# Softmax reciprocals of a chunked-attention block: transposed as 128x8 inside the probabilities' PSUM tile and spread over partitions by transfers on ScalarE's queue

## The chip, the core and the metric

The kernel runs on one core of one Trainium2 chip. The metric is the time of one execution in microseconds (us), measured on the device. TensorE (PE) multiplies and transposes into PSUM, VectorE (DVE) and ScalarE (ACT) work on PSUM and SBUF, GpSimd (POOL) works on SBUF, and SyncE (SP) issues almost all DMA transfers. In the program before the change ScalarE issues none.

## The reference

One layer: a shared input projection feeds a state-space mixer (SSM) and a chunked attention of 8 heads of 64; their outputs are normalised, projected and added, and a SwiGLU feed-forward layer follows. The part that matters here:

```python
scores = einsum(q, k) / sqrt(64) + bias          # each frame sees its 64-frame chunk and the 8 before
probs  = softmax(scores, axis=-1)
out    = einsum(probs, v)
```

The kernel leaves the probabilities unnormalised: it multiplies the exponentials with v and scales the product by one over the row sums afterwards.

## The kernel before, in words

The sequence of 2048 frames is cut into four blocks (`sb`) of 512. The eight heads are taken in four pairs (`pr`) of two (`hh`), and each head of a block in four query groups (`qp`) of 128 frames. That makes 128 steps, `steps[s] = (sb, pr, hh, qp)`. A pair ends with the step whose `(hh, qp)` is `(1, 3)`; this text calls that step b, and the place a boundary. There are 16 boundaries, named (block, pair) below.

In step s the loop at L1071 records, mostly in the order "sptf" (L1056/L1081):

- `scores` of step s (L937): the score matmuls into the PSUM tile `sc` (one buffer), the bias and row minimum on VectorE (L963, tile `mn`), and the exponential on ScalarE (L966), which also leaves the row sums in `sums` (tile `sm`).
- `pv_head` (L985), one step after the last transposes of a head: up to 16 matmuls of the transposed probabilities with v into a `pj` bank; ScalarE copies one half out (`yt`, L1006) and VectorE adds the other half into `ya` (L1007).
- `transp` of step s-2 (L970): up to five 128x128 transposes of the exponentials into the PSUM tile `pt`, of which there is one buffer; ScalarE rounds it out as `pth` (L982), and VectorE writes the remainder `ptl` (L983). The next step's transposes overwrite `pt`, so they wait for `ptl`.
- the background units ("f"): projections for q, k and v of the next block, the SSM and weight preparation, in small pieces between the steps. They keep PE busy. A planner spreads them over the steps by windows of steps.

PE's instructions stay in the order in which they are recorded. For the other engines a scheduler orders instructions when it builds the program; on the chip each engine then runs its list strictly in that order, and an instruction that waits holds up all that stand behind it.

At a boundary, before the change: at step b+3 `pv_head` takes the reciprocals of the 128x8 row sums (L993) and ScalarE writes them out 64 times each, as the 128x512 tile `rb` (L995). At step b+4 `pv_scale` (L1009) transposes `rb` by four 128x128 transposes into a `pj` bank (L1015), so that each reciprocal stands at its query's column on all 64 partitions of its head; VectorE multiplies `ya` by that bank (L1016), and SP stores `ya` to DRAM (L1017). On PE these four transposes stand directly ahead of the `pt` transposes of step b+4, which belong to probabilities of step b+2.

Transfers that SP and ScalarE issue share eight completion semaphores in rotation (DMAHW0 to DMAHW7 in the rows below). A transfer waits until the one before it on its semaphore has landed, whichever queue issued that.

Of the kernel before, what the change touches and what calls it, by code (L numbers as in the profile page):

```python
# [12 lines left out]
AF = mybir.ActivationFunctionType  # L13
# [91 lines left out]
def f32(ap):  # L105
    return ap.bitcast(F32)
# [629 lines left out]
def att_phase(k, ident, S, aw, x0, roots):  # L736

    tc, nc, io, pfs = k.tc, k.nc, k.io, k.pfs
    with ExitStack() as cx:
# [197 lines left out]
        def scores(st):  # L937
            sb, pr, hh, qp = st
            h = 2 * pr + hh
            if qp == 0:  # L940
                hd = st_head[sb, h] = Head()
                hd.nb = nbs.pop(h) if nbs else load_nb(h)
                hd.s = {}
                hd.p = None
            hd = st_head[sb, h]
            if qp == 1 and (sb, h) < (NSB - 1, H - 1):
                nbs[(h + 1) % H] = load_nb((h + 1) % H)
            q2h, q2l, k2 = qk[sb, pr][hh]
# [12 lines left out]
            if (hh, qp) == (0, 0):
                sums[sb, pr] = k.t(aa, "sm", [P, 2, 4], bufs=3)
            ins = nc.vector.tensor_tensor_reduce(  # L963
                s[:, :nk].rearrange("p (a b) -> p a b", a=nch), ps[:, :nch, :half],
                hd.nb[:, nk - 1 :: -1].rearrange("p (a b) -> p a b", a=nch), 1.0, 3e38, ALU.add, ALU.min, mn[:])
            nc.scalar.activation(s[:, :nk], s[:, :nk], AF.Exp, bias=mn[:], scale=-1.0, accum_out=sums[sb, pr][:, hh, qp : qp + 1])  # L966
            k.least = ins.ins
            hd.s[qp] = s, k0

        def transp(st):  # L970
            sb, pr, hh, qp = st
            hd = st_head[sb, 2 * pr + hh]
            if qp == 0:
                hd.p = k.t(aa, "pth", [P, 5, 4, P], F32R), k.t(aa, "ptl", [P, 5, 4, P], F32R)
            pth, ptl = hd.p
            s, k0 = hd.s.pop(qp)
            pt = k.t(psum, "pt", [P, 5, P], bufs=1)
            for kb in range(k0, qp + 5):
                k.ta.transpose(pt[:, kb % 5, :], s[:, (kb - k0) * P : (kb - k0 + 1) * P], ident[:])
            runs = [(0, 5)] if sb else ([(4, 5)] if qp == 0 else [(4, 5), (0, qp)])  # L980
            for a, b in runs:
                k.high = nc.scalar.copy(pth[:, a:b, qp, :], pt[:, a:b, :]).ins  # L982
                k.low = nc.vector.tensor_tensor(ptl[:, a:b, qp, :], pt[:, a:b, :], f32(pth[:, a:b, qp, :]), op=ALU.subtract).ins  # L983

        def pv_head(st):  # L985
            sb, pr, hh, _ = st
            h = 2 * pr + hh
            pth, ptl = st_head[sb, h].p
            if hh == 0:
                yas[sb, pr] = k.t(aa, "ya", [P, SB])  # L990
            if hh == 1:
                rs = k.t(aa, "rs", [P, 2, 4], bufs=2)
                nc.vector.reciprocal(rs[:], sums[sb, pr][:])  # L993
                rb = rbs[sb, pr] = k.t(aa, "rb", [P, 4, 2, HD])
                nc.scalar.copy(rb[:], rs[:].rearrange("p h i -> p i h").unsqueeze(3).to_broadcast([P, 4, 2, HD]))  # L995
            ya = yas[sb, pr]
            yp = k.t(psum, "pj", [P, 512], bufs=2)
            kbs = [4] + [kb for kb in (range(5, 8) if sb == 0 else (0, 1, 2, 3, 5, 6, 7))]
            for n, kb in enumerate(kbs):
                a, b = max(0, kb - 4), min(3, kb) + 1  # L1000
                vt = vts[4 * (sb - 1) + kb, h // 4][:, h % 4, :]
                for m, px in ((0, pth), (1, ptl)):
                    k.ta.matmul(yp[:, a * P : b * P], vt, px[:, kb % 5, a:b, :].rearrange("p a b -> p (a b)"),
                                     start=n == 0 and m == 0, stop=n == len(kbs) - 1 and m == 1)
            yt = k.t(aa, "yt", [P, SB])
            nc.scalar.copy(yt[:64], yp[64:128, :])  # L1006
            nc.vector.tensor_tensor(ya[hh * 64 : hh * 64 + 64, :], yp[0:64, :], yt[:64], op=ALU.add)  # L1007

        def pv_scale(st):  # L1009

            sb, pr, _, _ = st
            ya, rb = yas[sb, pr], rbs.pop((sb, pr))
            pb = k.t(psum, "pj", [P, 512], bufs=2)
            for i in range(4):
                k.ta.transpose(pb[:, i * P : (i + 1) * P], rb[:, i].rearrange("p h d -> p (h d)"), ident[:])  # L1015
            nc.vector.tensor_tensor(ya[:], ya[:], pb[:], op=ALU.mult)  # L1016
# [54 lines left out]
        for s in range(N + LAG + 2):  # L1071
# [9 lines left out]
            for o in TURNED.get(s % 32, ORDER) if s < N - 32 else ORDER:  # L1081
# [7 lines left out]
                        nc.gpsimd.tensor_copy(k.ys[GELU.index(s)].rearrange("p (c j) -> p c j", j=L), y[:, :, :64].rearrange("p j c -> p c j"))  # L1089
                elif o == "p" and LAG + 1 <= s < N + LAG + 1 and steps[s - LAG - 1][3] == 3:  # L1090
                    pv_head(steps[s - LAG - 1])
                elif o == "p" and s >= LAG + 2 and steps[s - LAG - 2][2:] == (1, 3):
                    pv_scale(steps[s - LAG - 2])
                elif o == "f":
                    for u in units[: None if s < GSTART else -1]:
                        u.advance(s)
# [853 lines left out]
def block_kernel(tc, io, phases="pusamf"):  # L1950
# [3 lines left out]
    with ExitStack() as cx:  # L1954
# [4 lines left out]
        def pp():  # L1959
# [1 line left out]

        S = {
            "u": k.t(dram, "u", [L, DS, NSB, NC // NSB]), "y": k.t(dram, "y", [L, DS, NC]),
            "ya": k.t(dram, "ya_s", [NSB, DS, SB]), "x1": k.t(dram, "x1", [D, SEQ]),
            "k": k.t(dram, "ks", [2, H, P, SB]), "nb": k.t(dram, "nbs", [H, 768]),
            "bst": k.t(dram, "bsts", [4, P, 8 * P]), "v": k.t(dram, "vs", [NPR, 2, 2, NS, 9 * CH]),
            "hc": k.t(dram, "hc", [2, 7, P, 4, 512]), "h": k.t(dram, "hs", [4, P, HALF]), "ws": k.t(dram, "wss", [12, P, 2, 1024]),
# [90 lines left out]
```

## Time and profile before

| | |
|---|---|
| median of 3 runs | 2187.09 us (2184.46 to 2187.53) |
| the profiled execution's own time | 2187.64 us |
| its span, first to last instruction | 2185.5 us |
| granted TensorE clock | 0.997 |
| attention steps | about 126 to 685 us of the span |

The profile is of one execution. Its span leaves 2.1 us of its own time outside. A row of a timeline gives the start in us from the span's start, the duration in us, engine, line, operation, output tile and input tiles, and the count; a bracket at the end gives idle time of that engine just before it and what ended that. A row of waits gives total, times and longest, in us. A row of a tile gives minimum, median and maximum duration in ns. Rows "SPq" are transfers on SP's queue; "to landing" is the time from a transfer's issue until all its data has arrived.

### The profile page before, as it was taken

Reading aid. Unit: us, or ns where it says so; the run is one execution under the profiler, and the core shown is the slowest. Engines: PE = TensorE matmul, PEld = TensorE weight load, DVE = VectorE, ACT = ScalarE, POOL = GpSimd, SP = SyncE. Lnnn points to the kernel's source line nnn. Section 1 sums busy time; section 2 is a strip of 40 time slices with the busy share of each in tenths; the row PEclk is TensorE's granted clock in tenths of the full one; section 3 lists DMA queues with packets and bytes.
Section 4 is the critical chain, followed back from the end, with each engine's and each line's share of the span. In section 5 each row is a group of like instructions: output and inputs, shape, how many; then the busy total and the mean of one; then the engine's idle time right before and its main releaser. Section 6 shows DMA issues by size and latency. Waiting matters only on the chain.

```text
span 2185.5 us, 30150 instructions
## 1 busy us (share of the span) xinstructions
PE 2144.4 (98%) x10606; PEld 1810.5 (83%) x10606; DVE 1535.0 (70%) x2680; ACT 1008.2 (46%) x1697; POOL 378.7 (17%) x849
## 2 busy tenths in 40 slices
PE   8998999999998999999999999999999999999998
PEld 7787898898887888888888888888888888888887
DVE  8767566666567667766776769766665587688785
ACT  7356466555586621533333345333333443353322
POOL 3367777676310000000000000000000100000000
PEclk9999999999999999999999999999999999999999
DMA  9788877965745346834554757555433476575552
GB/s 337 229 285 266 295 231 247 306 218 167 211 145 178 111 144 206 286 108 148 173 184 139 246 197 278 189 174 193 158 124 98 153 291 221 192 252 182 202 212 78
DMA packets 197592, 440.12 MB, mean 201 GB/s; under 512 B 20225, under 2 KB 37681, under 8 KB 190337
## 3 DMA queue, kind: packets, MB, share of 16 engines
q1 hardware_dynamic: 188816, 410.34, 56.1%
q0 software_dynamic: 8624, 27.86, 4.1%
q8 instruction: 83, 1.36, 0.3%
q14 instruction: 69, 0.56, 0.1%
HBM read 294.72 MB, written 135.29 MB: 197 GB/s over the span
## 4 chain that ended last, share of the span: by engine, by line
PE 89%; DVE 5%; DMA 2%; ACT 2%; issue 2%; SPq 0%; POOL 0%; DVEq 0%; ACTq 0%
PE X L83 22%; PE ps L83 22%; PE Y L83 11%; PE pf L83 10%; PE big L83 9%; PE W L83 5%; PE pj L83 4%; PE pt L86 2%; PE sc L83 2%; DVE ptl L983 1%; DVE w L182 1%; DVE lo L815 0%; DMA w<-wss 0%; DMA xt<-in_xp 0%; PE pp L83 0%
## 5 line engine op out<-in xcount | busy, mean ns | idle before, releaser
L83 PE MATMUL X<-hi,c 128*128 128x512 f32 x1408 | 448.9, 389 | 0.0
L83 PE MATMUL ps<-hd,hd 128*128 128x512 f32 (+1 forms) x1920 | 428.0, 384 | 0.0
L83 PEld LDWEIGHTS ps<-hd,hd 128*128 128x128 f32 x1920 | 353.4, 188 | 70.9 <-DVE hd L182 0.3
L83 PEld LDWEIGHTS X<-hi,c 128*128 128x128 f32 x1408 | 264.3, 188 | 55.2 <-DVE c L182 0.4
L83 PE MATMUL X<-lo,c 128*128 128x512 f32 x704 | 273.9, 389 | 0.0
L182 ACT CAST hd<-hd 128x1536 fp32r<-128x1536 f32 (+2 forms) x114 | 148.0, 1309 | 226.3 <-DMA hd<-hq 165.1
L83 PE MATMUL Y<-hi,c 128*128 128x512 f32 x696 | 222.2, 389 | 0.0
L182 DVE TENSOR_TENSOR hd<-hd 128x1536 fp32r<-128x1536 f32 (+2 forms) x114 | 174.8, 1539 | 32.3 <-ACT hd L182 31.9
L182 DVE TENSOR_TENSOR c<-S,c 128x512 fp32r<-128x512 f32 x175 | 120.2, 687 | 98.7 <-ACT c L182 98.4
L1620 ACT COPY u<-X 128x512 f32<-128x512 f32 x132 | 77.5, 587 | 191.6 <-PE X L83 191.5
L83 PE MATMUL big<-m,woh 128*128 128x512 f32 x512 | 160.1, 394 | 0.0
L1830 DVE TENSOR_TENSOR acc<-acc,ps 128x512 f32<-128x512 f32 x196 | 130.4, 681 | 42.1 <-PE ps L83 41.7
L182 ACT CAST c<-S 128x512 fp32r<-128x512 f32 x175 | 108.6, 622 | 107.5 <-PE Y L83 58.0
L83 PEld LDWEIGHTS X<-lo,c 128*128 128x128 f32 x704 | 132.2, 188 | 27.3
L83 PEld LDWEIGHTS Y<-hi,c 128*128 128x128 f32 x696 | 130.7, 188 | 27.3 <-DVE u L1624 0.2
L182 ACT CAST c<-raw 128x512 fp32r<-128x512 f32 x130 | 81.0, 623 | 152.2 <-PE Y L83 72.0
L83 PE MATMUL pf<-hi,w 128*128 128x512 f32 x416 | 148.2, 409 | 0.0
L1808 POOL DMA_DIRECT2D hd<-hq x4 | 2.5, 628 | 810.9 <-PE X L83 810.1
L83 PE MATMUL Y<-lo,c 128*128 128x512 f32 x348 | 135.4, 389 | 0.0
L983 DVE TENSOR_TENSOR ptl<-pt,pth 128x640 fp32r<-128x640 f32 (+3 forms) x152 | 98.1, 645 | 45.1 <-ACT pth L982 41.2
L966 ACT ACTIVATE s<-s,mn 128x640 f32<-128x640 f32 (+4 forms) x128 | 97.9, 765 | 50.7 <-DVE mn L963 47.8
L982 ACT CAST pth<-pt 128x640 fp32r<-128x640 f32 (+3 forms) x152 | 83.8, 551 | 76.3 <-PE pt L86 70.8
(514 smaller groups left out, 4280.6 us busy)
## 6 DMA issues: line engine op xcount, KB each, us to landing
w<-wss SPq DMA_DIRECT2D x36, 1024.0 KB, 6.9
hq<-g SPq DMA_DIRECT2D x140, 256.0 KB, 2.1
hd<-hq SPq DMA_DIRECT2D x35, 768.0 KB, 4.4
hd<-wc SPq DMA_DIRECT2D x35, 768.0 KB, 5.9
raw<-in_w_up SPq DMA_DIRECT2D x44, 512.0 KB, 4.0
raw<-in_w_gate SPq DMA_DIRECT2D x43, 512.0 KB, 3.7
wc<-px SPq DMA_DIRECT2D x66, 256.0 KB, 3.0
wss<-w SPq DMA_DIRECT2D x12, 1024.0 KB, 6.6
```

The costliest lines, as they stand in the source:

```text
L83: return self.tc.keep_in_program_order(self.tc.nc.tensor.matmul(*a, **b))
L86: return self.tc.keep_in_program_order(self.tc.nc.tensor.transpose(*a, **b))
L182: return nc.scalar.copy(hi, raw), nc.vector.tensor_tensor(lo, raw, f32(hi), op=ALU.subtract)
L966: nc.scalar.activation(s[:, :nk], s[:, :nk], AF.Exp, bias=mn[:], scale=-1.0, accum_out=sums[sb, pr][:, hh, qp : qp + 1])
L982: k.high = nc.scalar.copy(pth[:, a:b, qp, :], pt[:, a:b, :]).ins
L983: k.low = nc.vector.tensor_tensor(ptl[:, a:b, qp, :], pt[:, a:b, :], f32(pth[:, a:b, qp, :]), op=ALU.subtract).ins
L1620: self.kept = nc.scalar.copy(u[:], ps[:]).ins
L1808: k.ahead = nc.gpsimd.dma_start(f32(lo[:, d]), src[d].rearrange("g p c -> p g c")).ins
L1830: V.tensor_tensor(a, a, ps[:], op=ALU.add)
```

## The change

For 15 of the 16 boundaries (the last keeps the old way):

- The reciprocals are recorded at the end of step b+1 instead of step b+3 (`recip`).
- `pt` grows from `[P, 5, P]` to `[P, 6, P]` floats a partition. In `transp` at step b+2 a transpose of the 128x8 reciprocals goes into rows 0 to 7 of its sixth part. After `pth` and `ptl` of that step, ScalarE copies the 8x128 piece out (`rt`), and a transfer on ScalarE's own queue stores it to a small DRAM tensor `rs`.
- At the end of step b+3, behind that step's exponential on ScalarE (`issue_after(k.exp)`), two transfers on ScalarE's queue read it back (`spread`): each writes the 512 reciprocals of one head, a row of 2 KB, to all of that head's 64 partitions of `rb`.
- At step b+5 instead of b+4, VectorE multiplies `ya` by `rb`, now in SBUF, and SP stores `ya`.
- The four transposes of `rb` on PE and the 128x512 copy on ScalarE are gone.

```diff
+            k.exp = nc.scalar.activation(s[:, :nk], s[:, :nk], AF.Exp, bias=mn[:], scale=-1.0, accum_out=sums[sb, pr][:, hh, qp : qp + 1]).ins
...
+        def recip(st):
+            sb, pr, _, _ = st
+            rs = k.t(aa, "rs", [P, 2, 4], bufs=2)
+            nc.vector.reciprocal(rs[:], sums[sb, pr][:])
+            return rs
+
+        def spread(st):
+            sb, pr, _, _ = st
+            rb = rbs[sb, pr] = k.t(aa, "rb", [P, SB])
+            for hh in range(2):
+                src = S["rs"][pr % 2, hh * 4 : hh * 4 + 4]
+                with tc.issue_after(k.exp):
+                    nc.scalar.dma_start(rb[hh * 64 : hh * 64 + 64, :], bass.AP(src.tensor, src.offset, [[0, 64], [1, SB]]))
...
-            pt = k.t(psum, "pt", [P, 5, P], bufs=1)
+            pt = k.t(psum, "pt", [P, 6, P], bufs=1)
...
+            if (sb, pr) in rss:
+                k.ta.transpose(pt[:8, 5, :], rss[sb, pr][:].rearrange("p h i -> p (h i)"), ident[:])
...
+            if (sb, pr) in rss:
+                del rss[sb, pr]
+                rt = k.t(aa, "rt", [8, P])
+                nc.scalar.copy(rt[:], pt[:8, 5, :])
+                nc.scalar.dma_start(S["rs"][pr % 2], rt[:])
...
-            if hh == 1:
-                rs = k.t(aa, "rs", [P, 2, 4], bufs=2)
-                nc.vector.reciprocal(rs[:], sums[sb, pr][:])
+            if hh == 1 and (sb, pr) == (NSB - 1, 3):
+                rs = recip(st)
...
+            if (sb, pr) == (NSB - 1, 3):
+                pb = k.t(psum, "pj", [P, 512], bufs=2)
+                for i in range(4):
+                    k.ta.transpose(pb[:, i * P : (i + 1) * P], rb[:, i].rearrange("p h d -> p (h d)"), ident[:])
+                rb = pb
+            nc.vector.tensor_tensor(ya[:], ya[:], rb[:], op=ALU.mult)
...
+                elif o == "p" and LAG + 3 <= s < N and steps[s - LAG - 3][2:] == (1, 3):
+                    pv_scale(steps[s - LAG - 3])
...
+            if 1 <= s < N and steps[s - 1][2:] == (1, 3):
+                rss[steps[s - 1][:2]] = recip(steps[s - 1])
+            if 3 <= s < N and steps[s - 3][2:] == (1, 3):
+                spread(steps[s - 3])
```

What the scheduler makes of it, at three places. ScalarE's list before, around boundary (1, 0); `hi` and `q2h` belong to background units, `s` is an exponential, and the last two rows are the exponential of step b+4 and the `pth` of that step's transposes:

```order
L852 ACTIVATE q2h_3639<-pf_3647 64x512 [waits DMAHW7_49,PE_49]
L813 CAST hi_833_3767<-xt_3603 128x512 [waits DMAHW4_49,DVE_49]
L966 ACTIVATE s_3790,sm_3687<-s_3790,mn_3791 128x640 [waits DVE_49,Activation_49]
L1006 COPY yt_3815<-pj_3798 64x512 [waits PE_49]
L982 CAST pth_3818<-pt_3820 128x5x128 [waits PE_49,Activation_49]
L852 ACTIVATE q2h_3642<-pf_3647 64x512 [waits DMAHW6_49,PE_49]
L966 ACTIVATE s_3845,sm_3687<-s_3845,mn_3846 128x640 [waits DVE_49]
L982 CAST pth_3818<-pt_3856 128x5x128 [waits PE_49]
```

The same piece of ScalarE's list after:

```order
L852 ACTIVATE q2h_3640<-pf_3648 64x512 [waits DMAHW0_49,PE_49]
L1005 COPY rt_3752<-pt_3743 8x128 [waits DVE_49]
L813 CAST hi_836_3774<-xt_3604 128x512 [waits DMAHW7_49]
L1006 DMA rs_s_67<-rt_3752 8x128 [waits DMAHW1_49,Activation_49]
L966 ACTIVATE s_3797,sm_3688<-s_3797,mn_3798 128x640 [waits DVE_49]
L984 DMA rb_3843<-rs_s_67 64x512 [waits DMAHW6_49,DMAHW3_49,DMAHW1_49]
L984 DMA rb_3843<-rs_s_67 64x512 [waits DMAHW5_49]
L1028 COPY yt_3818<-pj_3801 64x512 [waits PE_49]
L1000 CAST pth_3821<-pt_3823 128x5x128 [waits PE_49]
L852 ACTIVATE q2h_3643<-pf_3648 64x512 [waits PE_49]
L1000 CAST pth_3821<-pt_3855 128x5x128 [waits PE_49]
L966 ACTIVATE s_3851,sm_3688<-s_3851,mn_3852 128x640 [waits DVE_49]
```

`rt` waits for VectorE's `ptl` (DVE), the store for `rt`, and the first read-back for the store's landing (DMAHW1). `yt` and `pth` of step b+3 stand behind the two read-backs, and the last `pth` now stands ahead of the last exponential.

VectorE's list before, around boundary (3, 0); the rows "mn" close a row minimum, and `q2l` belongs to a background unit:

```order
L1007 TENSOR_TENSOR ya_7268<-pj_7437,yt_7454 64x512 [waits Activation_49]
L983 TENSOR_TENSOR ptl_7458<-pt_7459,pth_7457 128x5x128 [waits DVE_49,Activation_49]
L963 ISA s_7486,mn_7487<-sc_7481,nba_99 128x640 [waits PE_49]
L963 ISA mn_7487 128x1
L858 SCALAR_TENSOR_TENSOR q2l_7331<-pf_7338,q2h_7330 64x512 [waits Activation_49]
L858 SCALAR_TENSOR_TENSOR q2l_7334<-pf_7338,q2h_7333 64x512 [waits DMAHW4_49]
L1016 TENSOR_TENSOR ya_7268<-ya_7268,pj_7490 128x512 [waits DVE_49,PE_49]
L983 TENSOR_TENSOR ptl_7458<-pt_7497,pth_7457 128x5x128 [waits Activation_49]
```

The same piece of VectorE's list after:

```order
L1029 TENSOR_TENSOR ya_7269<-pj_7440,yt_7457 64x512 [waits Activation_49]
L1001 TENSOR_TENSOR ptl_7461<-pt_7462,pth_7460 128x5x128 [waits DVE_49,Activation_49]
L1040 TENSOR_TENSOR ya_7269<-ya_7269,rb_7477 128x512 [waits DMAHW4_49,DMAHW3_49,DVE_49]
L963 ISA s_7492,mn_7493<-sc_7487,nba_100 128x640 [waits PE_49]
L963 ISA mn_7493 128x1
L858 SCALAR_TENSOR_TENSOR q2l_7332<-pf_7339,q2h_7331 64x512 [waits DMAHW2_49,Activation_49]
L858 SCALAR_TENSOR_TENSOR q2l_7335<-pf_7339,q2h_7334 64x512 [waits DMAHW0_49]
L1001 TENSOR_TENSOR ptl_7461<-pt_7496,pth_7460 128x5x128 [waits Activation_49]
```

The multiply, recorded a step later, stands in the list ahead of the row minimum, the two `q2l` and the second `ptl`, behind which it stood, and it waits for the two read-backs (DMAHW4 and DMAHW3).

SP's list before, around boundary (0, 1); `hi0x`, `lo0x` and `Bst` are operands of the SSM, `nbb` bias rows, `xt` a piece of the input:

```order
L606 DMA hi0x_2392<-u_64 128x512 [waits DMAHW2_49]
L606 DMA lo0x_2393<-u_64 128x512
L606 DMA Bst_2396<-bsts_70 128x512 [waits DMAHW4_49]
L585 DMA nbb_1554<-nbs_69 64x576 [waits DMAHW5_49]
L586 DMA nbb_1554<-nbs_69 64x576 [waits DMAHW6_49]
L787 DMA xt_2524<-in_xt 128x512 [waits DMAHW7_49,DVE_49]
```

The same piece of SP's list after:

```order
L606 DMA hi0x_2393<-u_64 128x512 [waits DMAHW0_49]
L606 DMA lo0x_2394<-u_64 128x512 [waits DMAHW1_49]
L606 DMA Bst_2397<-bsts_71 128x512 [waits DMAHW2_49]
L585 DMA nbb_1555<-nbs_70 64x576 [waits DMAHW3_49]
L586 DMA nbb_1555<-nbs_70 64x576 [waits DMAHW4_49]
L787 DMA xt_2527<-in_xt 128x512 [waits DMAHW7_49,DMAHW5_49,DVE_49]
```

And ScalarE's list after at that boundary, with a background `w`:

```order
L1005 COPY rt_2455<-pt_2445 8x128 [waits DVE_49]
L1006 DMA rs_s_67<-rt_2455 8x128 [waits DMAHW2_49,Activation_49]
L182 CAST w_2353<-raw_2293 128x512 [waits DMAHW5_49,DMAHW0_49,PE_49]
L1028 COPY yt_2500<-pj_2491 64x512 [waits PE_49]
L966 ACTIVATE s_2487,sm_2404<-s_2487,mn_2488 128x384 [waits DVE_49]
L1000 CAST pth_2503<-pt_2505 128x128 [waits PE_49]
L984 DMA rb_2533<-rs_s_67 64x512 [waits DMAHW2_49,DMAHW1_49]
```

The order of SP's transfers at this place is the same; what moved is the semaphore. The store of the reciprocals takes its turn on DMAHW2 just ahead of the load of `Bst`, which therefore waits until that store has landed, and everything on SP's queue stands behind `Bst`. Elsewhere on SP's queue the stores of `ya` move by one to four places.

More of the change, by code (lines that the diff above doesn't have):

```diff
@@ L965, in scores @@
                 hd.nb[:, nk - 1 :: -1].rearrange("p (a b) -> p a b", a=nch), 1.0, 3e38, ALU.add, ALU.min, mn[:])
-            nc.scalar.activation(s[:, :nk], s[:, :nk], AF.Exp, bias=mn[:], scale=-1.0, accum_out=sums[sb, pr][:, hh, qp : qp + 1])
+            k.exp = nc.scalar.activation(s[:, :nk], s[:, :nk], AF.Exp, bias=mn[:], scale=-1.0, accum_out=sums[sb, pr][:, hh, qp : qp + 1]).ins
             k.least = ins.ins
             hd.s[qp] = s, k0
+        def recip(st):
[10 more added lines that the diff above has]
+                    nc.scalar.dma_start(rb[hh * 64 : hh * 64 + 64, :], bass.AP(src.tensor, src.offset, [[0, 64], [1, SB]]))
         def transp(st):
@@ L1012, in pv_scale @@
             ya, rb = yas[sb, pr], rbs.pop((sb, pr))
[L1013 to L1016, printed above, removed]
+            if (sb, pr) == (NSB - 1, 3):
[4 more added lines that the diff above has]
+            nc.vector.tensor_tensor(ya[:], ya[:], rb[:], op=ALU.mult)
             (nc.gpsimd if (sb, pr) == (NSB - 1, 3) else nc.sync).dma_start(S["ya"][sb, pr * P : (pr + 1) * P, :], ya[:])
-        st_head, yas, sums, rbs = {}, {}, {}, {}
+        st_head, yas, sums, rbs, rss = {}, {}, {}, {}, {}
         steps = [(sb, pr, hh, qp) for sb in range(NSB) for pr in range(4) for hh in range(2) for qp in range(4)]
@@ L1091, in att_phase @@
                     pv_head(steps[s - LAG - 1])
-                elif o == "p" and s >= LAG + 2 and steps[s - LAG - 2][2:] == (1, 3):
+                elif o == "p" and LAG + 2 <= s and steps[s - LAG - 2] == (NSB - 1, 3, 1, 3):
                     pv_scale(steps[s - LAG - 2])
+                elif o == "p" and LAG + 3 <= s < N and steps[s - LAG - 3][2:] == (1, 3):
+                    pv_scale(steps[s - LAG - 3])
                 elif o == "f":
@@ L1963, in block_kernel @@
             "u": k.t(dram, "u", [L, DS, NSB, NC // NSB]), "y": k.t(dram, "y", [L, DS, NC]),
-            "ya": k.t(dram, "ya_s", [NSB, DS, SB]), "x1": k.t(dram, "x1", [D, SEQ]),
+            "ya": k.t(dram, "ya_s", [NSB, DS, SB]), "rs": k.t(dram, "rs_s", [2, 8, P]), "x1": k.t(dram, "x1", [D, SEQ]),
             "k": k.t(dram, "ks", [2, H, P, SB]), "nb": k.t(dram, "nbs", [H, 768]),
```

## The prediction

> **What bounds the kernel now.** I read the page's busy table first, then the attention stage by windows, then what PE waits for in it.
>
> ```profile
> span 2185.5 us, 30150 instructions
> PE 2144.4 (98%) x10606; PEld 1810.5 (83%) x10606; DVE 1535.0 (70%) x2680; ACT 1008.2 (46%) x1697; POOL 378.7 (17%) x849
> ...
> 126.00:240.00 114.00, 102.35 (x580) 86.32 (x579) 75.99 (x179) 66.58 (x177) 79.73 (x196) 0.99 0.83 273
> 240.00:600.00 360.00, 353.52 (x2200) 320.61 (x2199) 222.23 (x392) 213.00 (x431) 227.62 (x539) 1.00 0.75 237
> 600.00:685.00 85.00, 77.45 (x479) 67.99 (x478) 60.72 (x118) 67.23 (x109) 9.28 (x9) 0.98 0.43 141
> ...
> PEld pt L86 <- DVE ptl L983: 11.8, 19, 1.5
> PE pt L86 <- DVE ptl L983: 10.5, 16, 1.3
> ```
>
> A window row gives the stretch, then busy time (and count) of PE, its weight loads, DVE, ACT and POOL, the granted clock, the share of the 16 DMA engines and GB/s. PE is the bound: from 240 to 600 it idles 360.00 - 353.52 = 6.5 us. In the stretches before and after it idles 11.7 and 7.6 us. ScalarE (59% busy in the middle stretch) and VectorE (62%) have time left on average, but not everywhere: PE's transposes into `pt` wait for `ptl`, 10.5 us in 16 places. So time taken off PE counts nearly in full in the middle, and anything that makes `pth` or `ptl` late is paid by PE.
>
> The two waiting engines at boundary (1, 0), and PE beside them:
>
> ```profile
> 293.42 0.61 ACT L813 CAST hi<-xt 128x512 fp32r<-128x512 f32 x1
> 295.95 0.83 ACT L966 ACTIVATE s<-s,mn 128x640 f32<-128x640 f32 x1 [1.93 <-DVE mn L963]
> ...
> 296.90 0.58 ACT L1006 COPY yt<-pj 64x512 f32<-64x512 f32 x1
> 297.51 0.69 ACT L982 CAST pth<-pt 128x640 fp32r<-128x640 f32 x1
> ...
> 292.44 0.81 DVE L983 TENSOR_TENSOR ptl<-pt,pth 128x640 fp32r<-128x640 f32 x1
> ...
> 298.24 0.82 DVE L983 TENSOR_TENSOR ptl<-pt,pth 128x640 fp32r<-128x640 f32 x1
> ...
> 299.06 0.60 PE L86 MATMUL pj<-ident,rb 128*128 128x128 f32 x4
> 299.49 0.71 PE L86 MATMUL pt<-ident,s 128*128 128x128 f32 x5
> ```
>
> `ptl` of step b+3 ends at 299.06, and PE wants to overwrite `pt` at 299.49. What fills that gap of 0.43 us is just the four transposes that the change removes. There is no slack behind them.
>
> **The change part by part.** Signs: minus is time won.
>
> *PE.* Four transposes of `rb` take 299.49 - 299.06 = 0.43 us of the array's stream, 0.108 each; one transpose of the 128x8 reciprocals is added.
>
> ```profile
> L86 PEld LDWEIGHTS pj<-ident,rb x64: 138/140/143, 167.2 to 675.9; 128*128 128x128 f32 x64
> L995 ACT COPY rb<-rs x16: 603/617/619, 158.5 to 668.8; 128x512 f32<-128x512 f32 x16
> ...
> 126.00:240.00 114.00, 1.80 (x12) 1.50 (x12) 1.84 (x3) 0.99 0.83 273
> 240.00:600.00 360.00, 5.98 (x40) 4.96 (x40) 6.16 (x10) 1.00 0.75 237
> 600.00:685.00 85.00, 1.82 (x12) 1.41 (x12) 1.84 (x3) 0.98 0.43 141
> ...
> L982 ACT CAST pth<-pt 128x128 fp32r<-128x128 f32 x40 | 10.5, 262 | 18.8 <-PE pt L86 16.8 <-DVE ptl L983 1.7
> ```
>
> The trace has no transpose of 8 columns. Its bounds are 0 and 0.14 us (a 128-column weight load, 140 ns); I take 0.11, since the same 128 columns of the identity move through it. Net -0.32 us a boundary. The windows of `rb` alone count the groups: 12/4 = 3 boundaries in the first stretch, 40/4 = 10 in the middle, 3 in the last, of which the last boundary of all keeps the old way. I count the ten in full and the five others by half, since PE waits there for other things anyway: -0.32 x 12.5 = **-4.0**. All fifteen in full are -4.8, and this is the most that the change can win.
>
> The Trainium skill, page "TensorE: Matmul & The Clock Gate", section "LDWEIGHTS (loading the stationary operand)", says that a load's time goes with its columns, about columns/1.2 ns. That gives an estimate of 107 ns for 128 columns, where the trace has 140, and 7 ns for 8. If the load alone set the price, the sum would be lower by 15 x 0.10 = 1.5 us.
>
> *ScalarE's arithmetic.* The 0.617 us copy of `rb` goes. The 8x128 copy `rt` comes; the nearest row, a 128x128 cast out of `pt`, has 0.262 us. With the store's issue behind it the two about cancel, on an engine with a third of its time free. **0**. What is queued behind `rt` and its wait for `ptl` is only background work and the next exponential, which itself waits for VectorE (1.93 us idle at 295.95). The next `pt` transposes also wait for `rt` now, but up to 16 `pv` matmuls stand between.
>
> *ScalarE's queue.* The first read-back waits for the store's landing; behind it stand `yt` and `pth`, for which VectorE and PE wait. Neither ScalarE issues nor so small a store is in this trace. The nearest rows are SP's transfers of 64 rows:
>
> ```profile
> L866 SPq DMA_DIRECT2D q2h<-q2h x30: 462/483/654, 145.0 to 630.2; - x30
> ...
> DMA to landing us min/median/max: 2.2/4.3/8.6
> ...
> L586 SPq DMA_DIRECT2D nbb<-nbs x16: 451/588/1098, 129.8 to 640.4; - x16
> ...
> DMA to landing us min/median/max: 2.8/4.6/10.2
> ```
>
> At (1, 0): `ptl` ends at 293.25, `rt` takes till 293.5, the store goes out at about 293.6. Landing takes 2.2 at best, 4.3 at the median: it has landed at 295.8 or at 297.9. Two issues of 0.48 follow. `yt` could start at 296.90, so it is late by nothing or by 297.9 + 0.96 - 296.9 = 2.0 us, and without slack PE pays all of it. The store is 4 KB against 128 KB, so I take 2.8, nearer the minimum: landed 296.4, issued 297.4, 0.5 late. If the issues run beside the exponential (295.95 to 296.78) even this shrinks. Elsewhere the time from `ptl` to the exponential differs with the background work. By the same two rows at each of the fifteen I count nine boundaries under 3.1 us. In the three of them in block 0 `pth` or other work stands ahead of the read-backs, which leaves six, from (1, 0) to (3, 2), where `ptl` ends at 647.47 and the exponential starts at 649.51:
>
> ```profile
> 646.65 0.82 DVE L983 TENSOR_TENSOR ptl<-pt,pth 128x640 fp32r<-128x640 f32 x1 [0.78 <-ACT pth L982]
> ...
> 649.51 0.83 ACT L966 ACTIVATE s<-s,mn 128x640 f32<-128x640 f32 x1
> ```
>
> Six by half of 0.5 (some have slack): **+1.5**, bounds 0 and six by half of 2.0 = 6.
>
> The Trainium skill, page "DMA: Bandwidth & Descriptors", section "Anatomy of one DMA — SWDGE (gpsimd) path", speaks against a change like this: any semaphore wait of a transfer happens on the issuing sequencer, and a transfer has a fixed cost of about 2.0 us, mostly until the write is confirmed. Our smallest landing, 2.2 us, agrees. With its 2.0 us (an estimate for this queue) the store would be down at 295.6, before the exponential starts, and this term would be near 0.
>
> *VectorE's queue.* The multiply is as long as before, but waits for the read-backs and stands ahead of work that PE needs. At (3, 0):
>
> ```profile
> 585.90 0.83 ACT L966 ACTIVATE s<-s,mn 128x640 f32<-128x640 f32 x1 [0.92 <-DVE mn L963]
> ...
> 588.82 0.82 DVE L983 TENSOR_TENSOR ptl<-pt,pth 128x640 fp32r<-128x640 f32 x1
> 590.00 0.82 DVE L963 CUSTOM_DVE_ANT_0 s<-sc,nba 128x640 f32<-128x640 f32 x1 [0.35 <-PE sc L83]
> 590.75 0.08 DVE L963 DVE_READ_ACCUMULATOR2_ANT mn<- 128x1 f32 x1
> 590.75 1.40 DVE L858 SCALAR_TENSOR_TENSOR q2l<-pf,q2h 64x512 fp32r<-64x512 f32 x2
> 592.18 0.69 DVE L1016 TENSOR_TENSOR ya<-ya,pj 128x512 f32<-128x512 f32 x1
> 592.78 0.82 DVE L983 TENSOR_TENSOR ptl<-pt,pth 128x640 fp32r<-128x640 f32 x1
> ...
> 593.66 0.77 PE L86 MATMUL pt<-ident,s 128*128 128x128 f32 x5
> ```
>
> The second read-back goes out at about 585.9 + 0.5 = 586.4. With the bias rows' landing, 2.8 to 4.6 us (they too are 64 overlapping rows from DRAM), it is there at 589.2 to 591.0. VectorE arrives at 589.64. Then 0.69 for the multiply, 0.82, 1.40 and 0.82 for what now stands behind it: the second `ptl` ends at 593.4 to 594.7, against 593.60 before, and PE starts right behind it. So -0.2 to +1.1. I take a landing of 3.7: +0.3, and the 0.32 that PE won is lost too, together +0.6. Four more boundaries have the multiply shortly ahead of a row minimum, with no `q2l` between; 0.2 each. **+1.4**, bounds 0 and (1.1 + 0.3) + 4 x 0.5 = 3.4.
>
> *SP's queue.* At (0, 1) the load of `Bst` now waits for the store of the reciprocals:
>
> ```profile
> 192.82 0.55 DVE L983 TENSOR_TENSOR ptl<-pt,pth 128x384 fp32r<-128x384 f32 x1
> ...
> 194.49 0.44 SPq L606 DMA_DIRECT2D Bst<-bsts  x1
> ...
> 201.06 1.10 PE L83 MATMUL pj<-hi0x,Bst 128*128 128x256 f32 x4 [1.32 <-DMA Bst<-bsts]
> ```
>
> `ptl` ends at 193.37, the store goes out at about 193.7 and lands at 195.9 to 198.0, so `Bst` is issued 1.4 to 3.5 us later. PE waited 1.32 us for it already, so it is late by as much. I take **+2.0**, bounds 0 (if the time is regained before 240, where PE idles anyway) and 3.5. The store of `ya` goes out later with the multiply; what stands behind it on SP are loads well ahead of their use: 0.
>
> *Sum:* -4.0 + 1.5 + 1.4 + 2.0 = +0.9. The profiled execution took 2187.64 us, so 2188.5. The median of the runs shown is 0.55 lower, and the forecast is for the median: 2187.09 + 0.9 = **2188.0**.
>
> **The rivals.** What a measurement can tell from no change is about 0.2%, 4.4 us.
>
> - *All waits hide* (faster). The landings are near their minima and the issues run beside the exponential. Then -4.8: 2182.3. For it: small transfers, a queue of ScalarE's own. Against it: no slack at 299.06, and DMA engines 75% busy.
> - *ScalarE stands still* (slower). The store lands at the median of the nearest rows, 4.3 us. `yt`, `pth` and `ptl` are late and PE waits for `pt`. Its term is 6 then: 2187.09 - 4.0 + 6 + 1.4 + 2.0 = 2192.5. It decides from a landing of about 3 us; at (1, 0) each further 0.1 us is 0.1 us of PE. For it: a busy DMA stage; against it: 4 KB.
> - *VectorE takes it back* (no change). The other terms as forecast, VectorE's at its bound: -4.0 + 1.5 + 3.4 + 2.0 = +2.9, 2190.0.
> - *The shared semaphores stall SP* (slower). If not only `Bst` but loads at two more boundaries come 3 us late: +0.9 + 1.5 + 6 = +8.4, 2195.5. Against it: elsewhere SP reaches the transfer in question several us later than the store would land.
>
> **How the numbers follow.** Forecast 0.52, all hidden 0.17, ScalarE 0.20, VectorE 0.04, SP 0.07. Faster is the second, 0.17; the same is forecast and VectorE, 0.56; slower is ScalarE and SP, 0.27. The range runs from the first rival's 2182.3, below which lies what of that case I can't price, to all four terms at their upper bounds together, -4.0 + 6 + 3.4 + 3.5 = +8.9: 2196.0. I leave about 0.08 below it and 0.08 above.
>
> **What would show it.** Right: PE has 45 instructions fewer; `pt` waits for `ptl` grow by some 3 us in total; ScalarE shows about 0.5 us of waiting at the read-backs of short boundaries; PE's wait for `Bst` near 201 grows to about 3 us; stages behind 685 keep their length. Wrong: stores that land later than 3 us, a multiply that waits more than 2 us at most boundaries, or a middle stretch shorter by more than 4 us.

## The result, and the profile after

| | before | after |
|---|---|---|
| median (lowest to highest), five runs each | 2187.09 us (2184.46 to 2189.11) | 2219.75 us (2215.76 to 2225.07) |
| ratio, 95% interval | | 1.0144 (1.0129 to 1.0159) |
| the profiled execution, its span, its clock | 2187.64, 2185.5, 0.997 | 2215.76, 2213.9, 0.994 |

The kernel became 32.7 us slower; the forecast was 2188.0 with a range up to 2196.0. In the profile, 26.8 us of the 28.4 us by which the span grew are there by the end of the attention stage: the first matmul of the next stage starts at 676.1 before and at 702.9 after. So the attention stage, 126 to 685 us before, runs to 711.8 after. The page's busy table after, then that stage in one window of each kernel (columns as before: PE, its weight loads, DVE, ACT, POOL, granted clock, DMA share, GB/s):

```profile
span 2213.9 us, 30100 instructions
PE 2147.0 (97%) x10561; PEld 1806.6 (82%) x10561; DVE 1534.9 (69%) x2680; ACT 1003.5 (45%) x1697; POOL 382.2 (17%) x849
```

Before, and below it after:

```profile
126.00:685.00 559.00, 533.32 (x3256) 474.91 (x3255) 358.94 (x688) 346.81 (x715) 316.63 (x743) 0.99 0.72 230
```

```profile
126.00:711.80 585.80, 535.72 (x3212) 471.82 (x3211) 358.84 (x688) 341.94 (x715) 320.04 (x743) 0.98 0.72 226
```

PE's idle time in the stage is 559.00 - 533.32 = 25.7 us before and 585.80 - 535.72 = 50.1 us after: 24.4 more. Its busy time did not fall by the transposes that went, it rose by 2.4, at a lower granted clock (0.98 against 0.99). The waits from 126 to 720 us, PE's, then VectorE's, then SP's (total, times, longest):

```profile
PE pt L86 <- DVE ptl L1001: 31.5, 24, 4.3
PE sc L83 <- DVE mn L963: 7.3, 8, 1.7
...
PE pj L83 <- DMA Bst<-bsts: 2.5, 1, 2.5
...
DVE ya L1029 <- ACT yt L1028: 53.5, 24, 5.3
...
DVE ya L1040 <- DMA rb<-rs_s: 19.2, 11, 5.7
...
SPq L593 <- DMA rs_s<-rt: 7.7, 1, 7.7
```

PE waits for `ptl` 31.5 us where it was 10.5. VectorE stands 19.2 us at the multiply, and behind `yt` 53.5 us; that row (then L1007) had 41.2 before. The SP row is a load of `tms`, an SSM operand, held up by the store at (0, 0); PE shows no wait for it. The two new waits, one place each. ScalarE at boundary (2, 0):

```profile
454.87 0.29 ACTq L1006 DMA_DIRECT2D rs_s<-rt  x1
456.25 0.83 ACT L966 ACTIVATE s<-s,mn 128x640 f32<-128x640 f32 x1 [0.88 <-DVE mn L963]
456.99 0.19 ACT L966 ACTIVATION_READ_ACCUMULATOR s<-s,mn 128x1 f32 x1
460.41 1.11 ACTq L984 DMA_DIRECT2D rb<-rs_s  x2
461.56 0.58 ACT L1028 COPY yt<-pj 64x512 f32<-64x512 f32 x1 [4.39 <-DMA w<-wss]
462.17 0.69 ACT L1000 CAST pth<-pt 128x640 fp32r<-128x640 f32 x1
```

The store goes out at 454.87; ScalarE is free from 457.18, and the first read-back goes out at 460.41, 5.5 us behind the store. `yt` and `pth` stand behind it for 4.39 us (the row names another load as the releaser; with the store's wait taken away, below, the read-backs of this boundary go out 1.4 us behind the store, beside the exponential). PE there, and four windows:

```profile
460.09 0.31 PE L83 MATMUL sc<-k,q2l 128*128 128x320 f32 x1
463.77 1.33 PE L86 MATMUL pt<-ident,s 128*128 128x128 f32 x5 [3.38 <-DVE ptl L1001]
464.75 0.77 PE L83 MATMUL pf<-hi,w 128*128 128x512 f32 x1
465.33 0.63 PE L83 MATMUL pf<-lo,w 128*128 128x512 f32 x1
...
466.61 0.40 PE L83 MATMUL pf<-lo,w 128*128 128x512 f32 x1
```

```profile
456.90:460.40 3.50, 3.50 (x22) 2.94 (x20) 0.00 (x0) 0.27 (x2) 2.95 (x16) 1.00 0.88 341
460.40:463.80 3.40, 0.03 (x1) 0.03 (x1) 1.59 (x3) 1.87 (x3) 2.85 (x14) 0.91 0.62 188
463.80:466.80 3.00, 3.00 (x10) 2.61 (x11) 2.88 (x6) 1.51 (x3) 2.77 (x4) 0.53 0.40 120
466.80:470.00 3.20, 3.20 (x19) 2.80 (x19) 2.54 (x4) 0.89 (x2) 3.04 (x4) 1.00 0.49 157
```

PE stands for 3.38 us, and then, with work to do, has a granted clock of 0.53 for 3 us: the same 128x512 matmul takes 0.63 and then 0.40. This second price is in no term of the forecast. VectorE at boundary (1, 3):

```profile
420.99 0.82 DVE L1001 TENSOR_TENSOR ptl<-pt,pth 128x640 fp32r<-128x640 f32 x1
421.73 0.68 DVE L182 TENSOR_TENSOR lo0x<-raw,hi0x 128x512 fp32r<-128x512 f32 x1
425.60 0.69 DVE L1040 TENSOR_TENSOR ya<-ya,rb 128x512 f32<-128x512 f32 x1 [3.19 <-DMA rb<-rs_s]
426.21 0.82 DVE L963 CUSTOM_DVE_ANT_0 s<-sc,nba 128x640 f32<-128x640 f32 x1
426.95 0.08 DVE L963 DVE_READ_ACCUMULATOR2_ANT mn<- 128x1 f32 x1
426.95 0.82 DVE L1001 TENSOR_TENSOR ptl<-pt,pth 128x640 fp32r<-128x640 f32 x1
```

The multiply waits 3.19 us for the read-backs, and the row minimum and the second `ptl` wait with it.

### The profile page after: what moved, and what is told of

Same layout as the page of the kernel before. It is cut to its first block, busy times and chain, and to the rows that moved or that the text cites. A ratio compares the mean times of both kernels' runs of the same rounds, so it can differ in the third digit from the quotient of the medians.

```text
span 2213.9 us, 30100 instructions
## 1 busy us (share of the span) xinstructions
PE 2147.0 (97%) x10561; PEld 1806.6 (82%) x10561; DVE 1534.9 (69%) x2680; ACT 1003.5 (45%) x1697; POOL 382.2 (17%) x849
## 4 chain that ended last, share of the span: by engine, by line
PE 84%; DVE 5%; DMA 5%; ACT 2%; issue 2%; SPq 0%; ACTq 0%; DVEq 0%
PE ps L83 21%; PE X L83 21%; PE Y L83 11%; PE big L83 9%; PE pf L83 9%; PE W L83 5%; PE pj L83 3%; PE pt L86 2%; PE sc L83 2%; DMA rb<-rs_s 2%; DMA rs_s<-rt 1%; DVE ptl L1001 1%; DMA w<-wss 1%; DVE s L963 1%; DVE w L182 0%
## 5 line engine op out<-in xcount | busy, mean ns | idle before, releaser
L182 DVE TENSOR_TENSOR hd<-hd 128x1536 fp32r<-128x1536 f32 (+2 forms) x114 | 174.8, 1539 | 32.7 <-ACT hd L182 32.2
```

The costliest lines, as they stand in the source:

```text
L182: return nc.scalar.copy(hi, raw), nc.vector.tensor_tensor(lo, raw, f32(hi), op=ALU.subtract)
```

## The experiments

The first theory, **T1**: two waits make `ptl` late and PE pays for both, ScalarE's for the store and VectorE's for the read-backs. **T2**: the transfers cost by their traffic and by the semaphores that they share with SP's. **T3**: the cost is on PE's side, the sixth part of `pt` and the wait for `rt`. In the table each time is the median, the ratio is to runs of the kernel before on the same chip. The medians are of 4 to 12 runs each. "Clock" is an estimate of the time that a lower granted clock took, the mean over the runs of time x (1 - granted clock); the kernel before has 6.8 to 7.3 us in it, after 18.7.

| kernel | us | ratio (95%) | clock |
|---|---|---|---|
| no transfers | 2189.85 | 1.0015 (1.0004 to 1.0026) | 10.3 |
| no multiply wait | 2217.01 | 1.0131 (1.0116 to 1.0146) | 20.0 |
| no store wait | 2212.16 | 1.0114 (1.0098 to 1.0130) | 16.6 |
| nobody waits | 2194.16 | 1.0029 (1.0018 to 1.0041) | 7.3 |
| multiply behind | 2214.54 | 1.0122 (1.0105 to 1.0139) | 16.6 |
| both late | 2200.05 | 1.0058 (1.0038 to 1.0077) | 11.6 |
| product in rb | 2197.98 | 1.0043 (1.0026 to 1.0059) | 10.4 |
| old way in block 0 | 2191.75 | 1.0017 (1.0008 to 1.0026) | 9.2 |
| all on SP, multiply behind | 2205.45 | 1.0084 (1.0069 to 1.0099) | 14.9 |
| read-backs on SP, multiply behind | 2202.63 | 1.0070 (1.0054 to 1.0086) | 13.2 |
| read-backs on GpSimd, multiply behind | 2286.88 | 1.0448 (1.0431 to 1.0466) | 54.3 |
| before without transposes | 2192.20 | 1.0019 (1.0007 to 1.0031) | 9.6 |
| before with one of four | 2188.59 | 1.0008 (0.9997 to 1.0019) | 9.7 |

**No transfers.**

```diff
-                src = S["rs"][pr % 2, hh * 4 : hh * 4 + 4]
-                with tc.issue_after(k.exp):
-                    nc.scalar.dma_start(rb[hh * 64 : hh * 64 + 64, :], bass.AP(src.tensor, src.offset, [[0, 64], [1, SB]]))
+                nc.gpsimd.memset(rb[hh * 64 : hh * 64 + 64, :], 1.0)
...
-                nc.scalar.dma_start(S["rs"][pr % 2], rt[:])
+                pass
```

> The store and the two read-backs are left out at 15 boundaries, and GpSimd sets rb to 1.0 at the place of the read-backs, so the normalisation is left out there; the 8-column transpose, the copy rt and the place of the multiply stay. Theory T1 (two chained waits: the store's landing holds ScalarE's queue, the read-backs' landing holds VectorE's at the multiply): both waits go, what PE wins is left: 2182 to 2186. T2 (the transfers cost by their traffic and by the shared semaphores on SP's queue): also 2182 to 2186. T3 (the cost is on PE's side: the sixth part of pt, and pt waiting for rt): 2212 to 2220.

2189.85, 30 us below the changed kernel, with the sixth part of `pt` and the wait for `rt` still in it: T3 falls. It is also 4 to 8 us above what was expected of T1: even without transfers the change wins nothing. The last two experiments take that up.

**No multiply wait**, and **no store wait**: one wait is taken away, the transfers stay.

```diff
-            nc.vector.tensor_tensor(ya[:], ya[:], rb[:], op=ALU.mult)
+            nc.vector.tensor_tensor(ya[:], ya[:], rb[:] if (sb, pr) == (NSB - 1, 3) else ya[:], op=ALU.mult)
```

> The multiply takes ya for its second input in place of rb at 15 boundaries, so the normalisation is replaced by a square there; all transfers stay and nobody waits for the read-backs. T1: what VectorE's wait costs goes, some 15 to 20 us, ScalarE's wait for the store stays: 2198 to 2206. T2: all transfers and semaphores are there: 2215 to 2221. T3: 2215 to 2221.

```diff
-                src = S["rs"][pr % 2, hh * 4 : hh * 4 + 4]
+                src = S["nb"][hh, 0:SB]
```

> The read-backs take rows of the bias table in DRAM, written long before, so they don't wait for the store (which still goes out); the scale factors are not the reciprocals then. T1: ScalarE is no longer held (10 to 12 us), the read-backs go out 4 to 5 us earlier, so that the multiply waits less too: 2190 to 2204. T2: the same number of transfers and bytes: 2213 to 2221. T3: 2213 to 2221.

2217.01 and 2212.16: taking either away brings 3 to 8 us where T1 expected 14 or more. T1, with costs that add up, fell here, and T2 was ahead. The profiles spoke against T2. PE's waits without the multiply's wait, and the windows at boundary (1, 3) of that kernel, where ScalarE's queue stood:

```profile
PE pt L86 <- DVE ptl L1001: 33.1, 24, 4.5
PE sc L83 <- DVE mn L963: 5.9, 5, 1.9
```

```profile
417.80:421.20 3.40, 0.06 (x2) 0.01 (x1) 1.58 (x3) 1.79 (x3) 0.00 (x0) 0.86 0.90 339
421.20:427.30 6.10, 6.10 (x18) 4.97 (x19) 3.30 (x6) 2.03 (x4) 0.00 (x0) 0.52 0.77 274
427.30:431.00 3.70, 3.70 (x22) 3.27 (x21) 1.66 (x3) 2.35 (x5) 0.00 (x0) 1.00 0.58 114
```

One stand of 3.4 us, then half the clock for 6.1 us. VectorE's wait and PE's two, without the store's wait:

```profile
DVE ya L1040 <- DMA rb<-nbs: 26.4, 11, 5.5
...
PE pt L86 <- DVE ptl L1001: 23.2, 21, 3.0
...
PE sc L83 <- DVE mn L963: 12.1, 9, 3.1
```

The multiply waits longer than in the changed kernel (26.4 against 19.2), though its read-backs go out earlier. PE's waits for `ptl` and for the row minimum (`mn`) come to 31.5 + 7.3 = 38.8 us in the changed kernel, 39.0 without the multiply's wait and 35.3 without the store's. So **T1'**: each wait by itself makes PE stand about as long as both together, since at several boundaries one covers the other (at (2, 0) the multiply waits for nothing in the changed kernel; without the store's wait it waits there). In part the build's scheduler helps: with the store's wait gone it puts the multiply ahead of two `q2l` at (1, 0) and (2, 0). Both edits together decide between T1' and T2.

**Nobody waits** (both edits above; all 45 transfers stay).

> The last two single changes together: the read-backs take rows of the bias table and the multiply takes ya twice (so the normalisation is replaced by a square); all 45 transfers go out on ScalarE's queue at their places, and no engine waits for data from them. Theory T1' (either wait alone already makes ptl late, PE stands, and after a long enough stand its granted clock is 0.5 for some us; the waits overlap, so taking one away brings little): 2184 to 2192, and the stretches at clock 0.5 in the attention stage no more than before. T2 (the transfers themselves, their traffic and the shared semaphores): 2208 to 2218.

2194.16. T2 falls: with every transfer in place and nobody waiting, 25 of the 32 us (by the ratios) are gone, and the clock's share is back at that of the kernel before. T1' holds but for 2 us above its range: by the ratios it costs 3 us more than the kernel with no transfers at all, but the two intervals overlap.

**Multiply behind.** The multiply is held back behind work that PE needs, nothing else.

```diff
-            nc.vector.tensor_tensor(ya[:], ya[:], rb[:], op=ALU.mult)
+            with tc.issue_after(k.least) if (sb, pr) != (NSB - 1, 3) else nullcontext():
+                nc.vector.tensor_tensor(ya[:], ya[:], rb[:], op=ALU.mult)
```

> Nothing is left out: the multiply is issued behind the row minimum of step b+5 in VectorE's list; the transfers and ScalarE's list stay. T1': the multiply's wait goes, ScalarE's wait for the store's landing stays and is enough: 2206 to 2217. T1 with costs that add up: 2198 to 2206. T2: 2213 to 2221.

2214.54, as T1' has it: ScalarE's wait is enough. By itself this run doesn't tell T1' from T2, whose range holds it too; the run before did.

**Both late**: the multiply held back as in the last diff, read-backs at b+4, multiply at b+6.

```diff
-                elif o == "p" and LAG + 3 <= s < N and steps[s - LAG - 3][2:] == (1, 3):
-                    pv_scale(steps[s - LAG - 3])
+                elif o == "p" and LAG + 4 <= s < N and steps[s - LAG - 4][2:] == (1, 3):
+                    pv_scale(steps[s - LAG - 4])
...
-            if 3 <= s < N and steps[s - 3][2:] == (1, 3):
-                spread(steps[s - 3])
+            if 4 <= s < N and steps[s - 4][2:] == (1, 3):
+                spread(steps[s - 4])
```

> Nothing is left out: the read-backs go out a step later (b+4), the multiply is recorded a step later (b+6) and issued behind that step's row minimum. T1: store and read-backs have landed when they are waited for, so that neither ScalarE nor VectorE is held at most boundaries, and PE keeps what it wins: 2183 to 2191. T2 and T3: transfers and PE's work are unchanged: 2213 to 2221.

2200.05: most of the loss is gone with the transfers untouched, which speaks against T2 once more, but 9 us more is left than T1 expected. VectorE got another wait in it, for the landing of the store of `ya`, which the next pair overwrites:

```profile
DVE ya L1029 <- DMA ya_s<-ya: 14.2, 6, 3.0
```

**Product in rb**: both late, and the multiply writes to `rb` and SP stores it from there. **Old way in block 0**: that, with the way of the kernel before at the four boundaries of block 0.

```diff
...
+                yo = ya if (sb, pr) == (NSB - 1, 3) else rb
+                nc.vector.tensor_tensor(yo[:], ya[:], rb[:], op=ALU.mult)
-            (nc.gpsimd if (sb, pr) == (NSB - 1, 3) else nc.sync).dma_start(S["ya"][sb, pr * P : (pr + 1) * P, :], ya[:])
+            (nc.gpsimd if (sb, pr) == (NSB - 1, 3) else nc.sync).dma_start(S["ya"][sb, pr * P : (pr + 1) * P, :], yo[:])
```

> Nothing is left out: as the kernel with both read-backs and multiply a step later, but the product is written over rb and stored from there, so that ya is free for the next pair at the multiply and not at the landing of the store of ya. T1': the 14 us in which VectorE waited for that landing go; what is left over the kernel before is block 0 (Bst late behind the shared semaphore, and half the clock after it): 2188 to 2196.

> Nothing is left out: the last kernel, but the four boundaries of block 0 keep the way of the kernel before (eleven boundaries use the transfers). T1': no engine on PE's path waits for a landing and Bst is as before; what PE wins is left: 11 x 0.32 = 3.5 us at most: 2183 to 2189. T2 (transfers cost by themselves): above 2194.

2197.98 and 2191.75. The wait for the landing of `ya` is gone from the trace, and with it about 2 us, inside the intervals. Block 0 was worth 6 us. What is left is 1.0017 (1.0008 to 1.0026): the repaired change is still not faster than no change. It lies 2.8 us above the range of T1' and 2.3 below that of T2, so a small cost of the transfers themselves is not ruled out.

**Other queues**, with the multiply held back: all three transfers on SP's, the read-backs on SP's (this diff), the read-backs on GpSimd's.

```diff
-                with tc.issue_after(k.exp):
-                    nc.scalar.dma_start(rb[hh * 64 : hh * 64 + 64, :], bass.AP(src.tensor, src.offset, [[0, 64], [1, SB]]))
+                nc.sync.dma_start(rb[hh * 64 : hh * 64 + 64, :], bass.AP(src.tensor, src.offset, [[0, 64], [1, SB]]))
```

> Nothing is left out: store and read-backs go out on SP's queue, and the multiply is issued behind the row minimum of step b+5. T1': ScalarE and VectorE wait for neither landing at most boundaries; SP waits in their place, and its loads are issued well ahead of their use: 2184 to 2195. T2: as many transfers on the same semaphores, and SP stands still longer: 2210 to 2225.

> Nothing is left out: the store stays on ScalarE's queue, the two read-backs go out on SP's queue, and the multiply is issued behind the row minimum of step b+5. T1': 2184 to 2195, within 4 us of the kernel with all three transfers on SP's queue, since the store's issue makes nobody wait. T2: 2210 to 2225.

> Nothing is left out: the store stays on ScalarE's queue, the two read-backs go out on GpSimd's queue (with completion semaphores of its own), and the multiply is issued behind the row minimum of step b+5. T1': what stands still now is GpSimd, with the SSM's gathers behind it; if these have slack, 2184 to 2195; if not, X comes late and PE waits in pj: 2200 to 2215.

2205.45, 2202.63 and 2286.88, all above what was expected: a miss for "its loads are issued well ahead of their use". With the read-backs on SP, PE's waits for `ptl` fall to 15.6 us, but `Bst` comes late at (0, 1):

```profile
204.62 1.65 PE L83 MATMUL pj<-hi0x,Bst 128*128 128x256 f32 x3 [3.97 <-DMA Bst<-bsts]
```

```profile
200.60:204.60 4.00, 0.05 (x1) 0.00 (x0) 0.00 (x0) 0.00 (x0) 0.00 (x0) 0.79 0.83 302
204.60:211.00 6.40, 6.38 (x20) 5.35 (x21) 1.84 (x5) 3.94 (x12) 0.98 (x2) 0.60 1.00 376
```

On GpSimd's queue the read-backs stand behind that engine's own long work (at (0, 0) the first goes out at 192.00, 26.8 us behind the store), VectorE waits 96.0 us for them, and the clock's share is 54.3 us in the table. As the transfers were placed here, none of the queues had room to wait.

**Before without transposes**: the first term by itself.

```diff
...
-            for i in range(4):
+            for i in range(4 if rb else 0):
                 k.ta.transpose(pb[:, i * P : (i + 1) * P], rb[:, i].rearrange("p h d -> p (h d)"), ident[:])
-            nc.vector.tensor_tensor(ya[:], ya[:], pb[:], op=ALU.mult)
+            nc.vector.tensor_tensor(ya[:], ya[:], pb[:] if rb else ya[:], op=ALU.mult)
```

> The kernel before, without the reciprocals, the copy rb and the four transposes at the 15 boundaries; the multiply takes ya twice, so the normalisation is left out there. It measures the first term of the sum by itself, without transfers, new waits or a sixth part of pt. If what PE wins is as forecast: 2187.3 - 4.8 (all of 15 x 0.32 and the one transpose of 8 columns, 0.11 x 15 = 1.7, more) to 2187.3 - 4: 2181 to 2183.5. If other waits take it back, within 1.5 us of the kernel before.

2192.20, slower by 0.19% (0.07 to 0.31). The attention stage of it, to the same place as above, and PE's wait there:

```profile
126.00:686.20 560.20, 529.35 (x3198) 469.85 (x3197) 359.04 (x673) 338.41 (x700) 320.81 (x743) 0.99 0.72 229
```

```profile
PE pt L86 <- DVE ptl L983: 15.4, 18, 1.5
```

PE's busy time falls by 533.32 - 529.35 = 4.0 us, but its idle time grows from 25.7 to 30.9, and the wait for `ptl` alone by 4.9 (10.5 before). In this kernel the scheduler also moved the multiply (at (1, 0) it stands ahead of the row minimum and of two `q2l`, behind which it stood), and its two inputs are both in SBUF, so one more run left it where it was.

**Before with one of four**:

```diff
-            for i in range(4):
+            for i in range(1):
...
-            nc.vector.tensor_tensor(ya[:], ya[:], pb[:], op=ALU.mult)
+            nc.vector.tensor_tensor(ya[:].rearrange("p (a b) -> p a b", a=4), ya[:].rearrange("p (a b) -> p a b", a=4), pb[:, :P].unsqueeze(1).to_broadcast([P, 4, P]), op=ALU.mult)
```

> The kernel before with one transpose of rb at each boundary in place of four, and the multiply reading that quarter four times, still out of PSUM (three quarters of the queries get the wrong reciprocals, so the normalisation is changed at all 16 boundaries). PE loses 3 x 0.108 = 0.32 us a boundary, which is just the net that the first term of the forecast was made of; copy, multiply and its place stay. If PE's time is the kernel's time there: 2187 - 4.0 = 2183 (2181.5 to 2184.5). If PE only waits longer for ptl: 2186 to 2188. If it is slower by 3 or more, as without all four transposes, then the multiply out of SBUF and its place are not what took that gain back.

2188.59, no difference. In the profiled execution the attention stage did end 5.5 us earlier. Of these, 3.4 are the clock: the kernel before has two stretches at half the clock in the stage, where this one has none.

```profile
228.30:231.70 3.40, 3.40 (x13) 2.92 (x12) 1.54 (x4) 1.56 (x4) 2.85 (x15) 0.50 0.74 287
515.00:518.40 3.40, 3.40 (x11) 2.88 (x11) 2.99 (x6) 2.36 (x5) 0.00 (x0) 0.50 0.55 158
```

By 905 us only 0.9 of the 5.5 was left. Two stretches of 3.4 us at clock 0.5 came in behind the stage; one of them, and the same place before:

```profile
774.50:777.90 3.40, 3.40 (x10) 2.69 (x9) 3.40 (x19) 1.22 (x2) 0.00 (x0) 0.51 0.43 159
```

```profile
774.00:777.40 3.40, 3.15 (x22) 2.71 (x20) 1.59 (x3) 0.95 (x2) 0.00 (x0) 1.00 0.00 0
777.40:781.00 3.60, 3.60 (x21) 3.13 (x22) 3.13 (x16) 1.97 (x3) 0.00 (x0) 1.00 0.59 221
```

At both places PE idles 0.26 us between matmuls of one column; in one kernel the clock halves behind it, in the other it doesn't. Over all runs, the clock's share was 9.7 us here against 7.2, and the rest of the time 2179.2 against 2180.2 (each run's clock is listed to three places, so to 1.1 us). So of the gain of 4.0 about 1 is left once the clock is set aside. Whether the clock takes the rest in any kernel that gets there earlier, or by the chance of when PE arrives, stays open.

## Why the prediction was wrong

- *PE, -4.0.* The count of instructions came out, 45 fewer. Leaving the transposes alone out took 4.0 us off PE's busy time, where the forecast prices them at 15 x 0.43 = 6.5; one more stretch of 3.4 us at half the clock in that run (at 176.0) is 1.7 of the difference. The step that failed is "time taken off PE counts nearly in full in the middle": of two kernels that save such work and add no transfer, one was slower and one no different. What took the gain back is shown in part only: waits for `ptl` in the first, the clock in the second. The 8-column transpose was priced about right; its weight load takes 87 ns, between the bounds of 0 and 140:

```profile
L86 PEld LDWEIGHTS pt<-ident,rs x15: 86/87/87, 161.8 to 670.8; 128*8 128x8 f32 x15
L86 PE MATMUL pt<-ident,rs x15: 272/273/273, 161.9 to 670.9; 128*8 128x128 f32 x15
L1005 ACT COPY rt<-pt x15: 238/250/257, 164.9 to 673.9; 8x128 f32<-8x128 f32 x15
```

- *ScalarE's arithmetic, 0.* `rt` takes 0.250 us (0.262 was taken); nothing in the runs speaks against this.
- *ScalarE's queue, +1.5.* The step that failed: "The store is 4 KB against 128 KB, so I take 2.8, nearer the minimum". Where ScalarE stood, the first read-back went out 3.9 to 5.5 us behind the store in seven places, 4.6 at the median; at the same places of the kernel without the store's wait it was 1.2 to 2.7. The bytes were no guide to the landing, and it isn't one number: at (1, 1) the read-back went out 1.8 us behind the store. The rival "ScalarE stands still" had the mechanism, and the 4.3 us that it asked for was reached in five of the seven. Its 6 us were too few. With ScalarE's wait alone (multiply behind) the kernel is 27.3 us above the kernel before; 9.8 of these are the clock's by the table, which the rival left out, but the other 17.5, though they hold the smaller terms too, are far above 6. It took 1.0 us for each of six boundaries, and PE's single waits for `ptl` reached 4.3.
- *VectorE's queue, +1.4.* The landing of the read-backs, taken as 3.7 with an upper bound of 4.6, had a median of 5.0:

```profile
DMA to landing us min/median/max: 3.6/5.0/6.6
```

  The multiply waited 19.2 us in 11 places, where the term counted five. Each of the two queues alone is worth over 20 us over the kernel before (2212.16 and 2214.54), together 32.7. That they don't add up was not foreseen.
- *SP's queue, +2.0.* The mechanism was right: PE's wait for `Bst` went from 1.3 to 2.5 us. The load itself went out 5.0 us later (199.45 against 194.49), beyond the 3.5 of its bound, but PE got there later too. Behind the wait the clock was half for 3.4 us:

```profile
201.70:204.20 2.50, 0.01 (x1) 0.04 (x1) 1.14 (x3) 0.61 (x2) 0.00 (x0) 0.91 0.52 143
204.20:207.60 3.40, 3.40 (x10) 2.80 (x10) 0.69 (x1) 1.24 (x4) 0.00 (x0) 0.56 0.56 119
```

  With 0.44 x 3.4 = 1.5 for that, it comes to 2.7, inside the bounds.
- *What had no term.* The clock: 18.7 us after against about 7.2 before, by the estimate of the table 11.5 of the 32.7. The Trainium skill, page "TensorE: Matmul & The Clock Gate", section "HAM oscillation — how this bites in real kernels", says that an idle gap of PE beyond some 3.4 us throttles it again, so that the work behind the gap starts cold, at half the clock. The prediction used that page for a weight load and passed this rule by, though every slower rival was a stand of PE. The trace agrees on the half: 0.50 to 0.56 in the rows for 204.20, 228.30 and 515.00. It does not agree on the gap: 2.50 us was enough at 201.70, while a longer one at (1, 0) was followed by the full clock, as were two of 1.7 us at (1, 3):

```profile
308.10:311.00 2.90, 0.04 (x1) 0.05 (x1) 1.61 (x3) 1.87 (x3) 1.98 (x3) 1.00 0.89 206
311.00:314.40 3.40, 3.40 (x20) 2.99 (x21) 3.34 (x6) 1.51 (x3) 0.00 (x0) 1.00 1.06 203
```

  In the kernel before, the clock halved at 228.3 behind a stand of only 1.3 us. So the length of one stand doesn't settle it here; what else does wasn't tried. Each stretch at half the clock lasted 3.4 us or twice that.
- *The range.* Its top was all upper bounds together, 2196.0. They rested on two landings that were too short and on waits without the clock, so that the same two errors were in each of them, and the sum kept the -4.0 in full.
- *The rivals.* Of the three that lose time, "ScalarE stands still" and "VectorE takes it back" had their mechanisms right and came, each dearer than priced. Of "The shared semaphores stall SP" only `Bst` shows in PE's waits; the one other load there that PE waited longer for, `w`, went from 1.0 to 2.1 us. That the rivals could hold together was no case of its own, though one cause, landings later than the rows suggested, feeds the first two. "All waits hide" had nothing left to win, as the kernel without transfers shows.
- *What would show it.* "Stores that land later than 3 us" was named as a sign against the forecast, and is what came. "Stages behind 685 keep their length" held within 1.6 us.

## What to carry to other kernels

A transfer that an engine's queue waits for puts its whole landing on everything behind it: price it by landings of the same stage, not by its bytes. A stand of PE of two to four microseconds was often paid a second time in the clock, so in a stage where PE waits for one PSUM buffer a new wait is dear, and a saving of 0.3 us a boundary was worth nothing certain. Before such a change, leave the old work out without the new one: if that alone isn't faster, there is little for the rest to win.

## What the runs showed of the hardware

- A 4 KB store took about as long to be waited out (3.9 to 5.5 us where ScalarE stood, at most 1.8 us at (1, 1)) as a read-back of 64 partitions of 2 KB took to land (3.6 to 6.6 us), with the DMA engines 72% busy over the stage.
- A weight load of 8 columns takes 87 ns, one of 128 columns 140 ns.
- In the attention stage of the changed kernel PE's clock halved behind stands of 2.5 to 4.3 us, but stayed full behind one of 2.9 us. A 128x512 matmul took 0.63 us at half the clock, against 0.40.
- The 128x512 multiply took 677 to 689 ns with one input in PSUM. With both in SBUF most took the same, and some up to three times as long. In the kernel before without transposes:

```profile
L1017 DVE TENSOR_TENSOR ya<-ya x15: 681/685/2029, 170.9 to 654.4; 128x512 f32<-128x512 f32 x15
```

  What stretched these wasn't tried.
